# One core's decoder layer: q and k weights read in blocks of 128 input rows that alternate with v, sums of squares by products with ones, and GpSimd in the normalization of x

## The chip, the core and the metric

The kernel runs on one core of a Trainium2 chip as one program. The core has TensorE (PE, matrix products), VectorE (DVE), ScalarE (ACT), GpSimd (POOL) and SyncE (SP), which issues most of the transfers from device memory. Each engine works through its own instructions in program order and waits on semaphores for the others. The metric is the device time of one execution in microseconds (us); the median of several runs counts.

## The reference, cut to what matters

256 tokens of width 1024 go through one layer:

```python
mod = silu(c) @ mod_w + mod_b              # sh1, sc1, g1, sh2, sc2, g2
h   = rmsnorm(x, norm1_g) * (1 + sc1) + sh1
q, k, v, g_dn, r, conv_b, conv_c, conv_h, gate_a, gate_c = split(h @ w_in)
log_a = log_sigmoid(g_dn @ gate_w2 + gate_b) / 16
o = rmsnorm(gla_chunked(q, k, v, log_a)) * silu(r)      # 4 heads, chunks of 64
y = sigmoid(gate_a) * (o @ w_gla_out) + sigmoid(gate_c) * (conv(...) @ w_conv_out)
x = x + g1 * (y @ w_out)
x = x + g2 * hier_moe(rmsnorm(x, norm2_g) * (1 + sc2) + sh2)   # 64 experts
out = rmsnorm(x, final_norm_g)
```

All values are float32. A product of float32 quality is made from three products of split operands: each operand is cut into a high part and a low part, and high x high, high x low and low x high are added.

## The kernel before

**The work list.** The projections are 88 items, each a block of 128 partitions x 1024 float32 (512 KB) of weights. Items 0 to 15 are v, q and k; item 16 on are r, c, h, b, a, g, A, C and O, four blocks each half. For every item ACT casts the block to its high part (`split_h`, L304), DVE subtracts to get the low part (`split_l`, L311), and PE then runs the item's products: 12 of 512 columns for a v block (`mm_v`, L337), 24 of 256 columns for any other (`mm_half`, L328; `mm_blk`, L320). Splits are written five items ahead of the products (LA = 5), and the split buffers hold six items.

**The steps of x.** Eight steps k = 0 to 7, one for each 128 rows of the model width. `h_mod(k)` lets DVE multiply two blocks of mod_w by silu(c) and sum along the row (`mod_blk`, L226); ACT turns the sums into scale and shift, forms h (L256) and casts its high part (L257); DVE forms the low part (`h_lo`, L260). `xnorm(k)` multiplies x by the reciprocal root of its mean square (L245). In `prep(b)` a v item calls `h_mod`, then `split_l` of the item ahead of it, `split_h` of its own, `xnorm` of the next step and `h_lo`. Before, four v items (each with its step) are followed by two q and two k items, and that twice.

**The sums of squares.** DVE squares the first half of x and ACT the second; DVE adds the eight pieces by three additions, PE multiplies by a column of ones, ACT takes the root of the 128x2 result, DVE its reciprocal, and PE spreads it by two transposes.

**Buffers.** Weights come through a ring of 12 blocks: SP issues the next transfer when a block has been used. Accumulators lie in eight PSUM tiles, M0 to M3 and Z0 to Z3. `zt()` hands out the Z tiles in rotation, one for two items; a tile that comes round again can be written only when its last reader has finished. The tile of r's first two items (16 and 17) is read by `r_evac`, which ACT runs in loop 23 (`pre(b + 5)`), and the tile comes round again for item 24.

**The gate and the attention.** From `g_dn` a chain leads to the decays: `gate0`, `gate1` (PE, L380 and L390), absolute value and minimum, exp, ln (ACT), a running sum (DVE, L409), three more exps (`gate5`, `gate8`, ACT, L412, L422, L423). Then come `k_evac`, `q_evac` (DVE) and the attention (`gla_*`). A table of `at`, `first` and `pre` lines says in which loop b each piece is written. MODS spreads the later `mod_blk` calls over loops 19 to 65.

**The rest.** After the items come the router and 16 groups of experts, whose 403 MB of weights are read once.

Of the kernel before, what the change touches and what calls it, by code (L numbers as in the profile page):

```python
# [16 lines left out]
D = 1024  # L17
# [12 lines left out]
WARM = (4, 2)  # L30
XS = 38
# [63 lines left out]
def trunk_kernel(ctx: ExitStack, tc: tile.TileContext, xT: bass.AP, c: bass.AP, modw: bass.AP,  # L95
# [32 lines left out]
    worder = ["v0", "v1", "q", "k", "r0", "r1", "c0", "c1", "h0", "h1", "b0", "b1",  # L128
# [12 lines left out]
    for j in range(len(items) + LA):  # L141
        if j < len(items):
            kind, n, i = items[j]
            if kind[0] == "v":
                o = 2 * (kind == "vB")
# [60 lines left out]
    onesb = sm.tile([128, 128], BF, name="onesb")  # L206
    V.memset(onesb, 1.0)
# [36 lines left out]
    def xnorm(k):  # L244
        V.tensor_mul(xnt[:, k], xres[:, k], rstd1 if k else pr1[:, :TOK])  # L245
# [28 lines left out]
    rc = sm.tile([128, TT], F32, name="rc")  # L274
    S.activation(rc, ps[:, :, 0], AF.Sqrt, bias=epsc, scale=1.0 / D)
# [5 lines left out]
    V.reciprocal(rc, rc)  # L281
    pr1 = mt()
    for tt in range(TT):
        T.transpose(pr1[:, 128 * tt:128 * tt + 128], rc[:, tt:tt + 1].to_broadcast([128, 128]), ident)
    rstd1 = scr2
    S.copy(rstd1, pr1[:, :TOK])
    mod_blk(1, 0)
    xnorm(0)
# [34 lines left out]
    def mm_half(b, kind, i, pb):  # L323
        t = sp(b).rearrange("p s (j k m) -> p s j k m", j=2, k=4)
        for j in range(2):
            for k in range(4):
                for n, (ws, rs) in enumerate(PASSES):
                    T.matmul(pb[i % 2][:, j], t[:, ws, j, k], hl[rs][:, k + 4 * (i // 2)],  # L328
                             start=(kind[1] == "A" and j == 0 and k == 0 and n == 0),
                             stop=(kind[1] == "B" and j == 1 and k == 3 and n == 2), skip_group_check=True)  # L330
# [10 lines left out]
    def prep(b):  # L341

        kind, n, i = items[b]
        k = 4 * (kind == "vB") + i
        if kind[0] == "v":
            h_mod(k)
        if b > 0:
            split_l(b - 1)
        split_h(b)
        if kind[0] == "v":  # L350
            if k < KT - 1:
                xnorm(k + 1)
            h_lo(k)
# [177 lines left out]
    def o_split(h, f):  # L531
        if f is put_h and h == 0:
            L["ohl"] = big.tile([128, 2, KT, TOK], F32R, name="ohl", tag="T10")
        f(L["ohl"], L["o"][:, 2 * h:2 * h + 2], slice(2 * h, 2 * h + 2))


    def conv_tap0(s):
        for k in range(s.start, s.stop):
            S.activation(L["cu"][:, 1, k], L["cu"][:, 0, k], AF.Identity, scale=colt[:, CCW + 16 + k:CCW + 17 + k])

    def conv_taps(s):
        for k in range(s.start, s.stop):
            u, t = L["cu"][:, 0, k], L["cu"][:, 1, k]
# [24 lines left out]
    first(15, gate_abs)
    pre(15, gate_min)
    first(16, gate2)  # L570
    first(17, gate3)
    at(17, gate4)
    at(18, gate6)
    first(19, gate5)
    first(20, gate8)
    at(20, gate7)
    at(20, lambda: k_evac(0))
    at(21, lambda: k_evac(1))
    at(22, lambda: q_evac())
    at(22, gla_setup)  # L580
    at(24, gla_kst)
    at(25, gla_attn)
    first(25, gla_kst2)
    pre(26, gla_attn2, 0)
    pre(26, gla_attn2, 1)
    at(26, gla_state, 0, 1)
    first(27, gla_state2, 0)
    pre(27, gla_state2, 1)
    at(28, gla_state, 2)
    pre(29, gla_state2, 2)  # L590
    at(30, gla_o, 0)
    at(30, gla_o, 1)
    first(31, gla_o2, 0)
    first(31, gla_o2, 1)
    at(31, gla_o, 2)
    at(31, gla_o, 3)
    first(32, gla_o2, 2)
    first(32, gla_o2, 3)
    at(33, gla_ss)
    first(34, gla_ss2)  # L600
    pre(35, gla_ss3)
    at(36, gla_ss4)
# [101 lines left out]
    def evac(b, kind, n, i, ps):  # L704
        if kind[0] in "vqk":
            return
# [11 lines left out]
        elif kind == "c":  # L718
            if q == 0:
                pre(b + 5, conv_setup)  # L720
            pre(b + 5, c_evac, s, ps)
        elif kind == "h":
            V.tensor_mul(L["cu"][:, 0, s], L["cu"][:, 0, s], ps)
# [48 lines left out]
    for b in range(LA, nb):  # L772
        if items[b][0][0] not in "vqk":
            ahead.setdefault(b - (LA if b // 2 <= XS + 2 else LA - 2), []).append(b)
    for b, (kind, n, i) in enumerate(items):
        if i % 2 == 0 and kind[0] not in "vqk":
            ps = (zt(), zt()) if n == "O1" and i == 2 else zt()
        nxts = ahead.get(b, ())
        early = b + LA < nb and items[b + LA][0][0] in "vqk"
# [13 lines left out]
        if kind[0] == "v":  # L793
            mm_v(b, 4 * (kind == "vB") + i, pv)
        elif kind[0] in "qk":
            mm_half(b, kind, i, pq if kind[0] == "q" else pk)
# [375 lines left out]
def layouts(inp):  # L1172
# [21 lines left out]
    win += [w[:, 512 * i:512 * i + 512].reshape(2, 4, 128, 4, 128).transpose(2, 0, 3, 1, 4).reshape(128, 4096)  # L1194
# [37 lines left out]
```

## Time and profile before

| | |
|---|---|
| median of 3 runs (lowest to highest) | 1229.81 us (1229.1 to 1230.33) |
| the profiled execution's own time | 1230.86 us |
| its span, first to last instruction | 1229.0 us |
| busy: PE, DVE, ACT, POOL | 904.5, 379.5, 223.1, 3.9 us |
| moved by DMA | 478.36 MB, 389 GB/s over the span |

Busy time is an average over stages with different limits, so each stage is read by itself. A timeline row gives the start, the busy time of the merged instructions, the engine, the line, the operation, output<-input, the shape and the count; in brackets the idle time ahead of it and what ended it. A busy PE isn't PE at its peak: the rows merge products whose ends are modelled.

### The profile page before, as it was taken

Reading aid. Unit: us, or ns where it says so; the run is one execution under the profiler, and the core shown is the slowest. Engines: PE = TensorE matmul, PEld = TensorE weight load, DVE = VectorE, ACT = ScalarE, POOL = GpSimd, SP = SyncE. Lnnn points to the kernel's source line nnn. Section 1 sums busy time; section 2 is a strip of 40 time slices with the busy share of each in tenths; the row PEclk is TensorE's granted clock in tenths of the full one; section 3 lists DMA queues with packets and bytes.
Section 4 is the critical chain, followed back from the end, with each engine's and each line's share of the span. In section 5 each row is a group of like instructions: output and inputs, shape, how many; then the busy total and the mean of one; then the engine's idle time right before and its main releaser. Section 6 shows DMA issues by size and latency. Waiting matters only on the chain. (4 is left out here: it accounts for less than half of the span.)

```text
span 1229.0 us, 14492 instructions
## 1 busy us (share of the span) xinstructions
PE 904.5 (74%) x6135; PEld 475.6 (39%) x6135; DVE 379.5 (31%) x712; ACT 223.1 (18%) x370; POOL 3.9 (0%) x15
## 2 busy tenths in 40 slices
PE   6999999999788757576666666565756566757665
PEld 3999999998333313121212121221212111412111
DVE  7968799654421202020111111110202001202003
ACT  5674555443211001010101010100000000100002
POOL 0000000000000000000000000000000000000000
PEclk9999999999889888788978788888789887989787
DMA  9978859877999999999999999999999999999996
GB/s 361 406 240 290 269 186 344 342 273 294 401 404 427 428 428 428 428 428 428 427 428 428 428 427 427 428 428 428 427 428 427 429 427 427 426 428 428 427 415 226
DMA packets 56087, 478.36 MB, mean 389 GB/s; under 512 B 5969, under 2 KB 10193, under 8 KB 32338
## 3 DMA queue, kind: packets, MB, share of 16 engines
q1 hardware_dynamic: 54866, 475.56, 94.6%
q10 hardware_dynamic: 1152, 1.83, 0.4%
q8 instruction: 50, 0.82, 0.3%
q14 instruction: 19, 0.16, 0.0%
HBM read 476.31 MB, written 1.05 MB: 388 GB/s over the span
## 5 line engine op out<-in xcount | busy, mean ns | idle before, releaser
L993 PE MATMUL a<-unit,xt 128*32 128x512 f32 x1424 | 208.7, 717 | 103.6 <-DMA unit<-in_ew_dram 102.9
L993 PE MATMUL a<-unit,gt 128*32 128x512 f32 x672 | 112.2, 803 | 68.5 <-DMA unit<-in_ew_dram 65.6
L993 PEld LDWEIGHTS a<-unit,xt 128*32 128x32 f32 x1424 | 43.9, 122 | 253.7 <-DMA unit<-in_ew_dram 135.0
L320 PE MATMUL z<-hhl,sp 128*128 128x256 f32 x1152 | 140.4, 284 | 0.0
L320 PEld LDWEIGHTS z<-hhl,sp 128*128 128x128 f32 x1152 | 138.8, 192 | 1.1 <-issue 0.7
L969 ACT ACTIVATE xt<-m,modc,A 128x128 f32<-128x128 f32 x64 | 25.8, 454 | 534.3 <-PE m L965 534.3
L311 DVE TENSOR_TENSOR sp<-ring,sp 128x1024 fp32r<-128x1024 f32 x88 | 106.7, 1221 | 47.2 <-ACT sp L304 41.7
L993 PE MATMUL a<-ring,xt 128*32 128x512 f32 x624 | 88.7, 694 | 39.9 <-DMA ring<-in_ew_dram 39.8
L304 ACT CAST sp<-ring 128x1024 fp32r<-128x1024 f32 x88 | 90.9, 1047 | 96.2 <-PE z L320 65.2
L1021 DVE TENSOR_TENSOR wk<-wk,m 128x512 f32<-128x512 f32 (+1 forms) x66 | 44.4, 672 | 203.3 <-PE m L1020 203.2
L1011 DVE TENSOR_TENSOR xt<-a,xt 128x1024 f32<-128x1024 f32 (+2 forms) x18 | 19.9, 1106 | 273.5 <-PE a L993 264.3
L993 PEld LDWEIGHTS a<-unit,gt 128*32 128x32 f32 x672 | 22.2, 130 | 144.7 <-DMA unit<-in_ew_dram 91.4
L965 PEld LDWEIGHTS m<-Pm,wk 128*128 128x128 f32 x512 | 60.4, 196 | 21.4 <-issue 21.4
L965 PE MATMUL m<-Pm,wk 128*128 128x128 f32 x512 | 64.0, 284 | 4.7 <-DVE Pm L958 4.4
L1001 DVE TENSOR_TENSOR gt<-gt,a 128x512 f32<-128x512 f32 x16 | 11.0, 688 | 176.4 <-ACT gt L1000 176.4
L1020 PE MATMUL m<-xt,pwt 128*128 128x512 f32 (+1 forms) x132 | 62.8, 618 | 3.3 <-DVE xt L1011 3.3
L993 PE MATMUL a<-ring,gt 128*32 128x512 f32 x288 | 46.3, 774 | 25.2 <-DMA ring<-in_ew_dram 23.6
L226 DVE SCALAR_TENSOR_TENSOR xt<-ring,xt 128x1024 f32<-128x1024 f32 x48 | 58.6, 1221 | 0.6
L993 PEld LDWEIGHTS a<-ring,xt 128*32 128x32 f32 x624 | 18.4, 119 | 100.0 <-DMA ring<-in_ew_dram 58.2
L971 DVE TENSOR_SCALAR xt<-m,A,modc 128x128 f32<-128x128 f32 x64 | 23.3, 406 | 106.2 <-PE m L965 106.2
L1000 ACT ACTIVATE gt<-a 128x512 f32<-128x512 f32 x16 | 9.6, 597 | 229.6 <-PE a L993 229.6
L1020 PEld LDWEIGHTS m<-xt,pwt 128*128 128x128 f32 x132 | 25.1, 203 | 46.7 <-issue 36.7
(245 smaller groups left out, 620.1 us busy)
## 6 DMA issues: line engine op xcount, KB each, us to landing
unit<-in_ew_dram SPq DMA_DIRECT2D x131, 2048.0 KB, 39.1
ring<-in_ew_dram SPq DMA_DIRECT2D x54, 2048.0 KB, 39.1
ring<-in_win_dram SPq DMA_DIRECT2D x88, 512.0 KB, 6.6
ring<-in_modw_dram SPq DMA_DIRECT2D x48, 512.0 KB, 6.2
ring<-in_ew_dram SPq DMA_DIRECT2D x16, 512.0 KB, 7.7
unit<-in_ew_dram SPq DMA_DIRECT2D x4, 1024.0 KB, 34.8
unit<-in_ew_dram SPq DMA_DIRECT2D x4, 512.0 KB, 11.0
xt<-in_xT_dram SPq DMA_DIRECT2D x2, 512.0 KB, 5.0
```

What stands on the lines that cost most here:

```text
L226: V.scalar_tensor_tensor(scr, st.block("m", i, b), 1.0, cB, op0=OP.mult, op1=OP.mult, accum_out=modc[:, 4 * i + b:4 * i + b + 1])
L304: S.copy(sp(b)[:, 0], st.block("w", n, i))
L311: V.tensor_sub(t[:, 1], st.block("w", n, i), t[:, 0].bitcast(F32))
L320: T.matmul(ps, t[:, ws, k], rhs[rs][:, k], start=(clear and k == 0 and n == 0), stop=(k == KT - 1 and n == 2), skip_group_check=True)
L965: T.matmul(ps[:, j], h2[:, tt, f:f + 128], Pm[:, tt], start=(tt == 0), stop=(tt == 1))
L969: S.activation(xg[:, k], ps[:, j], AF.Identity, bias=B2[:, k:k + 1], scale=A2[:, k:k + 1])
L971: V.tensor_scalar(xg[:, k], ps[:, j], A2[:, k:k + 1], B2[:, k:k + 1], op0=OP.mult, op1=OP.add)
L993: T.matmul(ps[32 * j:32 * j + 32, 512 * hh:512 * hh + 512], lhsT[:, 32 * j:32 * j + 32], w[:, j, 512 * hh:512 * hh + 512], start=first, st ...
L1001: V.tensor_mul(gt, gt, ps[:, 512:1024])
L1011: V.tensor_mul(X["y"][:, c0:c1], ps[:, c0:c1], X["g2r"][:, c0:c1])
L1020: T.matmul(ps[:, :w], pwt[:, tt], X["y"][:, s], start=True, stop=True)
L1021: V.tensor_add(acc[:, tt, s], acc[:, tt, s], ps[:, :w])
```

## The change

- The q and k weights are laid out in one block for 128 input rows (as v's are), and the items alternate: v of step 0, qk of step 0, v of step 1, and so on. `mm_qk` multiplies all eight heads of q and k with one row of h. The pieces of the gate and the attention move three loops later (two at `o_norm` and `o_split`), and so do the small loads; `r_evac` and MODS keep their loops.
- The sums of squares come from eight float32 products of 256 columns with a matrix of ones, and root and reciprocal are then taken of 128x256. Three groups of products with ones in bfloat16 (4, 4 and 8 of 512 columns) are put ahead of, between and behind.
- `xnorm(k)` for k > 0 runs on GpSimd, all seven in a row as soon as the reciprocal is there.
- The transfers of c and of x's second half are issued by ACT.
- The convolution's tile `cu` lies in `gb` (T10), and `ohl` in T11. `gate1` skips one Z tile.

```diff
+START = (4, 4, 8)
-    for half, vn in (("A", "v0"), ("B", "v1")):
-        items += [("v" + half, vn, i) for i in range(4)]
-        items += [(n + half, n, i + 2 * (half == "B")) for n in "qk" for i in range(2)]
+    for k in range(KT):
+        items += [("v", f"v{k // 4}", k % 4), ("qk", f"qk{k // 4}", k % 4)]
...
-        nc.sync.dma_start(xres[:, 4 * i:4 * i + 4], xT[:, 4 * i:4 * i + 4])
+        (S if i else nc.sync).dma_start(xres[:, 4 * i:4 * i + 4], xT[:, 4 * i:4 * i + 4])
...
+    def start_warm(n):
+
+        for _ in range(n):
+            T.matmul(cold, onesb, onesb[:, None, :].to_broadcast([128, 4, 128]), start=True, stop=True)
...
     def xnorm(k):
-        V.tensor_mul(xnt[:, k], xres[:, k], rstd1 if k else pr1[:, :TOK])
+        (G if k else V).tensor_mul(xnt[:, k], xres[:, k], rstd1)
...
-    for n in (4, 2, 1):
-        V.tensor_add(xnt[:, 0:n], xnt[:, 0:n], xnt[:, n:2 * n])
-    ps = mt(2, 256)
-    for tt in range(TT):
-        T.matmul(ps[:, tt, 0:1], xnt[:, 0, 128 * tt:128 * tt + 128], onec, start=True, stop=True)
...
+    start_warm(START[1])
+    ps = mt()
+    for k in range(KT):
+        T.matmul(ps[:, :TOK], onesf, xnt[:, k], start=(k == 0), stop=(k == KT - 1))
+    start_warm(START[2])
+    rstd1 = scr2
+    S.activation(rstd1, ps[:, :TOK], AF.Sqrt, bias=epsc, scale=1.0 / D)
...
     mod_blk(0, 0)
...
     mod_blk(1, 0)
-    xnorm(0)
+    V.reciprocal(rstd1, rstd1)
+    for k in range(KT):
+        xnorm(k)
...
+    def mm_qk(b, kk):
+        t = sp(b).rearrange("p s (h m) -> p s h m", h=2 * H)
+        for h in range(2 * H):
+            pb = (pq, pk)[h // H][h % H // 2]
+            for n, (ws, rs) in enumerate(PASSES):
+                T.matmul(pb[:, h % 2], t[:, ws, h], hl[rs][:, kk],
+                         start=(kk == 0 and h % 2 == 0 and n == 0),
+                         stop=(kk == KT - 1 and h % 2 == 1 and n == 2), skip_group_check=True)
...
         split_h(b)
-        if kind[0] == "v":
-            if k < KT - 1:
-                xnorm(k + 1)
-            h_lo(k)
+        if kind == "v":
+            h_lo(b // 2)
...
         L["pg", i] = ps
+        rot["z"] += i
...
-    at(13, gate0)
-    first(14, gate0b)
-    at(14, gate1, 0)
-    at(14, gate1, 1)
+    at(16, gate0)
+    first(17, gate0b)
+    at(17, gate1, 0)
+    at(17, gate1, 1)
...
-    first(20, gate8)
+    first(23, gate8)
```

On DVE the rows of one step k in the middle of items 0 to 15 read so before (sp is a split buffer, t the normalized x or h, hhl the split h):

```order
L226 SCALAR_TENSOR_TENSOR xt,modc<-ring,xt 128x1024 x2
L311 TENSOR_TENSOR sp<-ring,sp 128x1024
L245 TENSOR_TENSOR t_119<-xt,scr_116 128x256
L260 TENSOR_TENSOR hhl<-t_119,hhl 128x256
L226 SCALAR_TENSOR_TENSOR xt,modc<-ring,xt 128x1024 x2
```

And so in the change, where lines are 4 to 8 further down:

```order
L234 SCALAR_TENSOR_TENSOR xt,modc<-ring,xt 128x1024 x2
L315 TENSOR_TENSOR sp<-ring,sp 128x1024
L268 TENSOR_TENSOR hhl<-t_124,hhl 128x256
L315 TENSOR_TENSOR sp<-ring,sp 128x1024
L234 SCALAR_TENSOR_TENSOR xt,modc<-ring,xt 128x1024 x2
```

The first split of a step is now that of the qk block of the step before; the normalization has left the row, and the split of the step's own v block stands ahead of the next step's two mod blocks, not behind them.

On ACT, at the end of the gate's chain, before (the first two rows are `gate5`, the next exps `gate8`; L702 is `r_evac`):

```order
L412 ACT_TABLE_LOAD
L412 ACTIVATE t_158<-t_158 128x1024
L304 CAST sp<-ring 128x1024
L422 ACTIVATE t_158<-t_158 128x1024
L423 ACTIVATE gb<-gb 128x1024
L304 CAST sp<-ring 128x1024 x4
L702 ACT_TABLE_LOAD
L702 ACTIVATE t_158<-z 128x512
```

The same place in the change:

```order
L414 ACT_TABLE_LOAD
L414 ACTIVATE t_180<-t_180 128x1024
L308 CAST sp<-ring 128x1024
L424 ACTIVATE t_180<-t_180 128x1024
L425 ACTIVATE gb<-gb 128x1024
L308 CAST sp<-ring 128x1024
L703 ACT_TABLE_LOAD
L703 ACTIVATE t_180<-z 128x512
```

Four casts, that is three to four items of PE, stood between `gate8` and `r_evac`; now one does.

On PE from `gate1` (L390) to the attention's first transposes (L440), before; L328 is an item of q or k, L320 of r and what follows, 24 products each:

```order
L390 MATMUL z<-e_71 128x256 x4
L328 MATMUL m<-hhl,sp 128x256 x48
L320 MATMUL z<-hhl,sp 128x256 x192
L440 MATMUL m<-ident,gb 128x128 x8
L320 MATMUL z<-hhl,sp 128x256 x24
```

And in the change from the last qk item on, with `gate0` as L381, `gate1` as L391 and the transposes as L442:

```order
L332 MATMUL m<-hhl,sp 128x256 x24
L381 MATMUL z<-t_124,e_71 32x256 x8
L324 MATMUL z<-hhl,sp 128x256 x24
L391 MATMUL z<-e_71 128x256 x4
L324 MATMUL z<-hhl,sp 128x256 x240
L442 MATMUL m<-ident,gb 128x128 x8
```

Ten items stood between `gate1` and the end of item 23; now seven do (17 to 23). The transposes stood ahead of item 24; now they stand three items later.

## Rows read from the trace of the kernel before

**Rows 1.** Stretches: length, busy us of PE, PEld, DVE, ACT, POOL, PEclk, DMA share, GB/s

```profile
160.00:180.00 20.00, 20.00 (x169) 20.00 (x169) 18.68 (x29) 10.24 (x13) 0.00 (x0) 1.00 0.61 192
340.00:700.00 360.00, 248.70 (x1578) 79.00 (x1576) 55.00 (x124) 21.39 (x47) 0.00 (x0) 0.84 1.00 426
```

**Rows 2.** Timeline of PE, 0 to 110 us

```profile
2.44 3.75 PE L264 MATMUL m<-e,onesf 1*128 1x512 f32 x4 [2.44 <-DMA e<-in_c_dram]
...
16.05 2.07 PE L337 MATMUL z<-sp,hhl 128*128 128x512 f32 x4 [2.99 <-ACT sp L304]
...
32.31 11.68 PE L328 MATMUL m<-hhl,sp 128*128 128x256 f32 x96
43.82 11.07 PE L337 MATMUL z<-sp,hhl 128*128 128x512 f32 x48
...
57.69 1.07 PE L380 MATMUL z<-t,e 128*32 128x256 f32 x16
...
61.66 1.89 PE L390 MATMUL z<-e 128*128 128x256 f32 x8
63.20 6.10 PE L328 MATMUL m<-hhl,sp 128*128 128x256 f32 x48
69.14 23.20 PE L320 MATMUL z<-hhl,sp 128*128 128x256 f32 x192
92.18 1.04 PE L440 MATMUL m<-ident,gb 128*128 128x128 f32 x8
```

**Rows 3.** Timeline of all engines, 0 to 45 us: the start

```profile
7.17 1.06 ACT L267 ACTIVATE t<-xt 128x1024 f32<-128x1024 f32 x1 [0.35 <-DMA xt<-in_xT_dram]
...
13.09 0.37 ACT L286 COPY scr<-m 128x256 f32<-128x256 f32 x1 [1.05 <-PE m L284]
...
13.49 0.42 DVE L245 TENSOR_TENSOR t<-xt,m 128x256 f32<-128x256 f32 x1
...
14.95 1.04 ACT L304 CAST sp<-ring 128x1024 fp32r<-128x1024 f32 x1
```

**Rows 4.** The same timeline: one step of items 0 to 3

```profile
19.69 1.22 DVE L226 SCALAR_TENSOR_TENSOR xt<-ring,xt 128x1024 f32<-128x1024 f32 x1
...
22.10 1.22 DVE L311 TENSOR_TENSOR sp<-ring,sp 128x1024 fp32r<-128x1024 f32 x1
...
23.49 1.04 ACT L304 CAST sp<-ring 128x1024 fp32r<-128x1024 f32 x1
23.62 0.43 DVE L260 TENSOR_TENSOR hhl<-t,hhl 128x256 fp32r<-128x256 f32 x1
23.96 1.22 DVE L226 SCALAR_TENSOR_TENSOR xt<-ring,xt 128x1024 f32<-128x1024 f32 x1
```

**Rows 5.** Lines L508 and L433: ns least/median/most, first and last start

```profile
L508 DVE RECIPROCAL scr<-scr x1: 1745/1745/1745, 140.3 to 140.3; 128x256 f32<-128x256 f32 x1
...
L433 POOL MEMSET gc<- x1: 958/958/958, 80.6 to 80.6; 128x1024 f32 x1
```

**Rows 6.** Timeline of ACT, 56 to 93 us

```profile
80.44 1.28 ACT L412 ACT_TABLE_LOAD   x1 [3.91 <-DVE t L409]
...
84.59 1.04 ACT L423 ACTIVATE gb<-gb 128x1024 f32<-128x1024 f32 x1
...
90.49 1.28 ACT L702 ACT_TABLE_LOAD   x1
91.79 0.60 ACT L702 ACTIVATE t<-z 128x512 f32<-128x512 f32 x1
```

**Rows 7.** Stretches around the router, columns as in group 1

```profile
324.00:326.00 2.00, 0.94 (x12) 0.04 (x4) 1.79 (x9) 0.57 (x2) 0.00 (x0) 1.00 0.97 401
326.00:328.00 2.00, 0.00 (x0) 0.00 (x0) 1.79 (x16) 0.00 (x0) 0.00 (x0) 0.95 0.96 410
336.00:338.00 2.00, 2.00 (x13) 0.34 (x6) 0.00 (x0) 0.00 (x0) 0.00 (x0) 0.50 1.09 467
338.00:340.00 2.00, 2.00 (x19) 2.00 (x20) 0.04 (x1) 0.81 (x2) 0.00 (x0) 0.99 0.93 397
```

More of the change, by code (lines that the diff above doesn't have):

```diff
@@ L125, in fl @@
         return t.rearrange("p a b -> p (a b)")
-    worder = ["v0", "v1", "q", "k", "r0", "r1", "c0", "c1", "h0", "h1", "b0", "b1",
+    worder = ["v0", "v1", "qk0", "qk1", "r0", "r1", "c0", "c1", "h0", "h1", "b0", "b1",
               "a0", "a1", "g0", "g1", "A0", "A1", "C0", "C1", "O0", "O1"]
@@ L143, in trunk_kernel @@
             kind, n, i = items[j]
-            if kind[0] == "v":
-                o = 2 * (kind == "vB")
+            if kind == "v":
+                o = 2 * int(n[1:])
                 blocks += [(("m", o, i), modw[o, :, 1024 * i:1024 * i + 1024]),
@@ L193, in trunk_kernel @@
     G.iota(jp, pattern=[[1, 128]], base=0, channel_multiplier=-1)
+    onesb = sm.tile([128, 128], BF, name="onesb")
+    V.memset(onesb, 1.0)
     onesf = sm.tile([128, 128], F32, name="onesf")
     V.memset(onesf, 1.0)
+    cold = zt(512)
+    def start_warm(n):
+        for _ in range(n):
+            T.matmul(cold, onesb, onesb[:, None, :].to_broadcast([128, 4, 128]), start=True, stop=True)
+    start_warm(START[0])
     epsc = sm.tile([128, 1], F32, name="epsc")
@@ L205, in trunk_kernel @@
     V.tensor_scalar(tri, jp, 0.0, None, op0=OP.is_gt)
-    onesb = sm.tile([128, 128], BF, name="onesb")
-    V.memset(onesb, 1.0)
     io = sm.tile([128, 128], F32, name="io")
@@ L280, in trunk_kernel @@
     mod_blk(0, 0)
[L281 to L286, printed above, removed]
     mod_blk(1, 0)
-    xnorm(0)
+    V.reciprocal(rstd1, rstd1)
+    for k in range(KT):
+        xnorm(k)
     spt = [big.tile([128, 2, 2, 1024], F32R, name="sp", tag=t) for t in SPLIT]
@@ L321, in mm_blk @@
                          stop=(k == KT - 1 and n == 2), skip_group_check=True)
[L323 to L330, printed above, removed]
+    def mm_qk(b, kk):
[6 more added lines that the diff above has]
+                         stop=(kk == KT - 1 and h % 2 == 1 and n == 2), skip_group_check=True)
     def mm_v(b, kk, pv):
@@ L343, in prep @@
         kind, n, i = items[b]
-        k = 4 * (kind == "vB") + i
-        if kind[0] == "v":
-            h_mod(k)
+        if kind == "v":
+            h_mod(b // 2)
         if b > 0:
@@ L349, in prep @@
         split_h(b)
-        if kind[0] == "v":
-            if k < KT - 1:
-                xnorm(k + 1)
-            h_lo(k)
+        if kind == "v":
+            h_lo(b // 2)
     def small_loads():
@@ L532, in o_split @@
         if f is put_h and h == 0:
-            L["ohl"] = big.tile([128, 2, KT, TOK], F32R, name="ohl", tag="T10")
+            L["ohl"] = big.tile([128, 2, KT, TOK], F32R, name="ohl", tag="T11")
         f(L["ohl"], L["o"][:, 2 * h:2 * h + 2], slice(2 * h, 2 * h + 2))
@@ L538, in conv_tap0 @@
         for k in range(s.start, s.stop):
-            S.activation(L["cu"][:, 1, k], L["cu"][:, 0, k], AF.Identity, scale=colt[:, CCW + 16 + k:CCW + 17 + k])
+            S.activation(cu1[:, k], cu0[:, k], AF.Identity, scale=colt[:, CCW + 16 + k:CCW + 17 + k])
     def conv_taps(s):
         for k in range(s.start, s.stop):
-            u, t = L["cu"][:, 0, k], L["cu"][:, 1, k]
+            u, t = cu0[:, k], cu1[:, k]
             for j in (1, 0):
@@ L559, in pre @@
         todo.setdefault((i, "pre"), []).append((f, a))
-    at(1, small_loads)
-    at(12, late_loads)
-    first(12, lambda: v_evac())
-    at(13, gate0)
-    first(14, gate0b)
-    at(14, gate1, 0)
-    at(14, gate1, 1)
[L568 to L574, printed above, removed]
-    first(20, gate8)
[L576 to L602, printed above, removed]
+    at(8, small_loads)
+    at(14, late_loads)
+    first(15, lambda: v_evac())
+    at(16, gate0)
+    first(17, gate0b)
+    at(17, gate1, 0)
+    at(17, gate1, 1)
+    first(18, gate_abs)
+    pre(18, gate_min)
+    first(19, gate2)
+    first(20, gate3)
+    at(20, gate4)
+    at(21, gate6)
+    first(22, gate5)
+    first(23, gate8)
+    at(23, gate7)
+    at(23, lambda: k_evac(0))
+    at(24, lambda: k_evac(1))
+    at(25, lambda: q_evac())
+    at(25, gla_setup)
+    at(27, gla_kst)
+    at(28, gla_attn)
+    first(28, gla_kst2)
+    pre(29, gla_attn2, 0)
+    pre(29, gla_attn2, 1)
+    at(29, gla_state, 0, 1)
+    first(30, gla_state2, 0)
+    pre(30, gla_state2, 1)
+    at(31, gla_state, 2)
+    pre(32, gla_state2, 2)
+    at(33, gla_o, 0)
+    at(33, gla_o, 1)
+    first(34, gla_o2, 0)
+    first(34, gla_o2, 1)
+    at(34, gla_o, 2)
+    at(34, gla_o, 3)
+    first(35, gla_o2, 2)
+    first(35, gla_o2, 3)
+    at(36, gla_ss)
+    first(37, gla_ss2)
+    pre(38, gla_ss3)
+    at(39, gla_ss4)
     for h in range(H):
-        at(38 + 2 * h, o_norm, h)
-        at(40 + 2 * h, o_split, h, put_h)
-        at(41 + 2 * h, o_split, h, put_l)
+        at(40 + 2 * h, o_norm, h)
+        at(42 + 2 * h, o_split, h, put_h)
+        at(43 + 2 * h, o_split, h, put_l)
     for b, ms in mod_at.items():
@@ L663, in trunk_kernel @@
     ps = None
-    def conv_setup():
-        L["cu"] = big.tile([128, 2, KT, TOK], F32, name="cu", tag="T11")
+    cu1, cu0 = (gb[:, 2 * i:2 * i + 2].rearrange("p a h t -> p (a h) t") for i in range(2))
     def c_evac(s, ps):
-        S.copy(L["cu"][:, 0, s], ps)
+        S.copy(cu0[:, s], ps)
     def q_evac():
@@ L682, in b_evac @@
             L["chl"] = big.tile([128, 2, KT, TOK], F32R, name="chl", tag="T9")
-        x = L["cu"][:, 1, 2 * q:2 * q + 2]
+        x = cu1[:, 2 * q:2 * q + 2]
         V.tensor_mul(x, x, ps)
@@ L687, in b_high @@
         s = slice(2 * q, 2 * q + 2)
-        put_h(L["chl"], L["cu"][:, 1, s], s)
+        put_h(L["chl"], cu1[:, s], s)
     def b_low(q):
         s = slice(2 * q, 2 * q + 2)
-        put_l(L["chl"], L["cu"][:, 1, s], s)
+        put_l(L["chl"], cu1[:, s], s)
         if q == 3:
-            st.free("T11")
+            st.free("T10")
     def v_evac():
@@ L704, in evac @@
     def evac(b, kind, n, i, ps):
-        if kind[0] in "vqk":
+        if kind in ("v", "qk"):
             return
@@ L718, in evac @@
         elif kind == "c":
[L719 to L720 removed]
             pre(b + 5, c_evac, s, ps)
         elif kind == "h":
[L723 removed]
+            V.tensor_mul(cu0[:, s], cu0[:, s], ps)
             at(b + 1, conv_tap0, s)
@@ L736, in evac @@
             if q == 3:
-                st.free("T10")
+                st.free("T11")
         elif kind == "C":
@@ L772, in trunk_kernel @@
     for b in range(LA, nb):
-        if items[b][0][0] not in "vqk":
+        if items[b][0] not in ("v", "qk"):
             ahead.setdefault(b - (LA if b // 2 <= XS + 2 else LA - 2), []).append(b)
     for b, (kind, n, i) in enumerate(items):
-        if i % 2 == 0 and kind[0] not in "vqk":
+        if i % 2 == 0 and kind not in ("v", "qk"):
             ps = (zt(), zt()) if n == "O1" and i == 2 else zt()
         nxts = ahead.get(b, ())
-        early = b + LA < nb and items[b + LA][0][0] in "vqk"
+        early = b + LA < nb and items[b + LA][0] in ("v", "qk")
         run((b, "first"))
@@ L783, in trunk_kernel @@
         for nxt in nxts:
-            if items[nxt - 1][0] == "kB":
+            if items[nxt - 1][0] == "qk":
                 split_l(nxt - 1)
@@ L792, in trunk_kernel @@
         run(b)
[L793 to L796, printed above, removed]
+        if kind == "v":
+            mm_v(b, b // 2, pv)
+        elif kind == "qk":
+            mm_qk(b, b // 2)
         else:
@@ L1193, in layouts @@
            for i in range(2)]
-    win += [w[:, 512 * i:512 * i + 512].reshape(2, 4, 128, 4, 128).transpose(2, 0, 3, 1, 4).reshape(128, 4096)
+    win += [w[512 * i:512 * i + 512, 0:1024].reshape(4, 128, D).transpose(1, 0, 2).reshape(128, 4096)
             for i in range(2)]
```

4 lines of the change are left out of this document (1 added, 3 removed).

## The prediction

> **What bounds the kernel now.** I read the stretches first. From about 340 us on the transfers run at 426 GB/s with a DMA share of 1.00, while PE is busy for 249 of 360 us; before that, as in 160 to 180 us, PE is busy for the whole stretch and DMA for 61% [rows 1]. So the projections are bound by PE and the experts by their transfers, and these wait for ring blocks and tiles that the projections free. Whatever moves the end of the projections moves the long transfer stretch by as much. The question is only when PE gets through its list.
>
> The timeline of PE answers it for the kernel before. PE starts item 0 at 16.05 us, ends item 15 at 69.14, with `gate0` (57.69) and `gate1` (61.66) inside, and ends item 23 at 92.18 [rows 2]. A v item takes 12 x 11.07 / 48 = 2.77 us, an item of 24 products of 256 columns 24 x 23.20 / 192 = 2.90 [rows 2]. Sixteen items would take 8 x (2.77 + 2.90) = 45.4; with the 1.07 of `gate0` and the 1.54 from 61.66 to 63.20 of `gate1` 48.0. PE took 53.1 from 16.05 to 69.14, so its early stalls and slow products hold 5.1 us. That is what alternating can win at most, if PE starts no earlier.
>
> **The start.** I call X0 the moment at which `xnorm(0)` starts: 13.49 before. From there to the end of the first cast is 2.50 (14.95 + 1.04) [rows 3], and that path stays. In the change PE first runs four products with ones (about 1.9, by the four at 16.05 in 2.07), so the products of c end near 6.8 instead of 6.19 [rows 2]. The second silu and ACT's square (1.06, ended at 8.23 before [rows 3]) follow. Four more products with ones and the eight of the sums come next. `gate1` took 1.89 for four float32 products of 256 columns [rows 2], so eight take 3.8 and the four with ones 0.9: they end near 11.3. The root of 128x256 on ACT goes by the copy of that shape, 0.37 [rows 3]. The reciprocal of 128x256 takes 1.75 [rows 5]; it was 128x2 before. X0 is 11.3 + 0.4 + 1.7 = 13.4, no gain. The bounds: 11.9 if PE catches up with ACT's square, 18.3 if all of it runs at half the clock. I take a value near the lower one, since PE works almost without a pause from 1.2 us on. What the three additions and two transposes cost is given back by the reciprocal.
>
> **The pace of the steps.** In the step before, the first mod block starts at 19.69, the first split at 22.10 (two mod blocks, 2.41), ACT's cast of the v block at 23.49, `h_lo` at 23.62 [rows 4]. Put the change's order on these: the cast of v ends 4.84 after the step's start; DVE, which has done `h_lo` by 4.36, waits for it and splits v from 4.88. The split takes 1.14 to the next start (1.22 less some 0.08 of overlap, as `h_lo`'s 0.43 gives 0.34 to the next start [rows 4]). The next step starts after 6.02. PE needs 2.77 + 2.90 = 5.67, so DVE and ACT's chain set the pace, not PE. The normalization that leaves DVE wins nothing here: `h_lo` waits for ACT's cast of h, and 0.42 of DVE lay under that wait.
>
> The first mod block of step 1 starts at X0 + 2.50 + 0.04 + 1.14 = X0 + 3.68. Step 7 starts six paces later, at X0 + 39.8. Behind it come the split of step 6's qk block (ends 2.41 + 1.22 = 3.63 later), 22 of its 24 products (2.66), item 14 (2.77) and item 15 (2.90): item 15 ends at X0 + 51.8 = 65.2. A low clock at the first items is hidden, since PE is ahead of DVE's pace by 0.35 a step.
>
> **Seven items instead of ten.** `gate0` (1.07) and item 16 (2.90) end at 69.2. Then `gate1` (1.54) and items 17 to 23 (7 x 2.90): PE could start item 24 at 91.0, where it stood at 92.18 before. The front is worth 1.1 us.
>
> But item 24 writes the Z tile that item 16 filled, and `r_evac` must have read it. Before, ACT finished `gate8` at 84.59 + 1.04 = 85.63, 23.97 after `gate1` began at 61.66; the chain waited only at its start for PE and once for DVE's running sum (3.91) [rows 2, 6]. Four casts later `r_evac` ran from 90.49 to 92.39; the attention's transposes filled PE from 92.18 on, so the wait was covered [rows 2, 6]. In the change the chain starts with `gate1` at 69.2 and takes the same 23.97, since the same operations in the same order depend on the same offsets of PE's items. One cast (1.04 [rows 4]), the table load (1.28) and the silu (0.60) follow: 69.2 + 26.9 = 96.1. PE reaches item 24 at 91.0 and finds nothing else to do: 5.1 us of idle time. The cover, three items and the transposes, is gone. Queued behind on ACT are the casts of items 29 and 30, which PE doesn't need yet.
>
> **What follows the idle time.** [...] I charge 4 us of work at half the clock, 2.0 lost; the bounds are 0 and 5.1, half of the low stretch from 327.8 to 338, and since part of that stretch was idle I stay below the middle. Further on, two mod blocks (2.41 [rows 4]) now stand on DVE ahead of the attention's masked copy, for which PE waits; bounds 0 and 2.4, I take 0.5, since most of an item of PE covers them.
>
> **GpSimd.** No row has a product on GpSimd. Its largest memset, four times as wide, took 0.96 [rows 5]. A fourth of it, 0.24, and all of it are the bounds for one of the seven; a product reads two operands and writes one, so I take 0.7. Their results are needed a step apart and are in time either way. If they don't disturb DVE, the price is 0; if each holds DVE up for its length at the upper bound, 6.7. Three of the seven fall into DVE's waits before step 1, and of the other four I charge half: 1.4.
>
> The seven operations lie where DVE sets the pace, so a hold-up would be paid in full. [...]
>
> The moved transfers of c and x cost ACT two more issues, before its first work. `cu` and `ohl` trade tiles, and both are freed at the same items as before; I cost that at nothing, because the same number of tiles is freed in the same order.
>
> **The sum.** -1.1 (front) + 5.1 (item 24) + 2.0 (clock) + 0.5 (attention) + 1.4 (GpSimd) = +7.9. Against the profiled execution's own 1230.86 that is 1238.8; that execution is 1.05 above the median of the runs shown, so I predict 1229.81 + 7.9 = 1237.7.
>
> **The rivals.**
> - *The chain is in time.* If `r_evac` ends within 21.8 of `gate1`'s start instead of 26.9, item 24 doesn't wait and the clock stays. This takes away 7.1: 1230.6, not slower; with X0 at its lower bound 1229.1, and from there on each further part that costs less than charged (GpSimd 1.4, attention 0.5) carries it below 1227.3, to faster. For it: the margin before can't be read closely, since the transposes hid it. Against it: three table loads and the scan are in the chain whatever PE does. Chance 0.25, of which 0.13 end faster by over 0.2% and 0.11 within it.
> - *The wait without the clock.* PE idles 5.1 but keeps its clock: 1235.7. The clock at the router fell after a shorter pause, which speaks against it. Chance 0.15.
> - *GpSimd holds DVE up in full.* Each of the seven products takes DVE's turn for its 0.7 us, 4.9 in all, or up to 6.7: 1241.2 to 1243. Against it: DVE waits for ACT twice in a step. [...] Chance 0.15.
> - *PE sets the pace of the steps.* If DVE's step is 5.67 or less, item 15 ends up to 2.1 earlier: 1235.6, or 1234.2 if GpSimd's price is hidden too. Chance 0.10. The change would then win what alternating is able to win, and lose it at item 24.
>
> The forecast itself keeps 0.35; its own range, with the bounds of X0, the clock and GpSimd, is 1234 to 1241.
>
> **How the numbers follow.** Fast and slow cases lie on one side except for the chain in time, so the range reaches down into it: 1228.5 to 1242 leaves out about 0.13 below and 0.06 above. A difference of 0.2% (2.5 us) is about what a measurement of this kernel can tell from none. Faster: 0.13. Within 0.2%: 0.12, almost all from the chain in time. Slower: 0.75.
>
> **What the profile of the changed kernel would show.** X0 near 13.4 and the reciprocal at 1.7; steps that start 6.0 apart; item 15's end near 65 to 66.5; PE idle for some 5 us ahead of item 24 with ACT's `r_evac` as the releaser, ACT having gone from `gate8` through one cast to the table load; a granted clock of 0.50 after it; the experts' transfers at 426 GB/s, as long as before and some 8 later. The prediction is wrong if there is no idle time between items 16 and 40, if X0 lies beyond 15, or if the transfers start later without PE being later.

## The result

The changed kernel takes 1237.91 us (median of 4; 1237.8 to 1240.42) against 1229.45 (median of 4), 8.5 us more; the ratio is 1.0072, 95% interval 1.006 to 1.0084. The profiled execution took 1237.93, its span is 1236.1. The forecast was 1237.7. The main wait and its mechanism were right, one term had the wrong sign, and that the figure fits so well is chance, as the parts show.

The two stretches of [rows 1], after the change (columns as there):

```profile
160.00:180.00 20.00, 20.00 (x163) 19.79 (x162) 18.23 (x28) 9.22 (x13) 0.00 (x0) 1.00 0.51 154
340.00:700.00 360.00, 247.12 (x1592) 81.26 (x1596) 57.86 (x137) 23.70 (x52) 0.00 (x0) 0.86 1.01 428
```

The limits are the same: PE in the projections, transfers in the experts. PE's timeline, with the rows that answer to [rows 2]:

```profile
8.39 4.75 PE L280 MATMUL m<-t,onesf 128*128 128x256 f32 x16
...
18.09 5.49 PE L341 MATMUL z<-sp,hhl 128*128 128x512 f32 x12 [3.23 <-ACT sp L308]
...
68.78 1.07 PE L381 MATMUL z<-t,e 128*32 128x256 f32 x16
...
72.75 1.89 PE L391 MATMUL z<-e 128*128 128x256 f32 x8
74.29 20.50 PE L324 MATMUL z<-hhl,sp 128*128 128x256 f32 x168
99.53 10.33 PE L324 MATMUL z<-hhl,sp 128*128 128x256 f32 x72 [4.75 <-ACT t L703]
109.70 1.03 PE L442 MATMUL m<-ident,gb 128*128 128x128 f32 x8
...
118.19 2.74 PE L467 MATMUL m<-t,gc 64*128 64x256 f32 x16
```

Item 15 ends at 68.78, items 16 to 23 and the gate's products end at 94.8, and there PE stops: item 24 waits 4.75 us for `r_evac` (L703). ACT's timeline shows why it is late (compare [rows 6]):

```profile
91.44 1.28 ACT L414 ACT_TABLE_LOAD   x1 [3.85 <-DVE t L411]
...
95.60 1.04 ACT L425 ACTIVATE gb<-gb 128x1024 f32<-128x1024 f32 x1
96.54 1.03 ACT L308 CAST sp<-ring 128x1024 fp32r<-128x1024 f32 x1
97.59 1.28 ACT L703 ACT_TABLE_LOAD   x1
98.88 0.60 ACT L703 ACTIVATE t<-z 128x512 f32<-128x512 f32 x1
```

One cast stands between `gate8` and the table load, and `r_evac` ends at 99.48, 26.7 after `gate1` began at 72.75. At the end of the pause the granted clock falls from 1.00 to 0.50 (column PEclk) and comes back:

```profile
98.00:100.00 2.00, 0.47 (x2) 0.47 (x3) 2.00 (x4) 1.99 (x3) 0.00 (x0) 0.85 0.48 166
100.00:102.00 2.00, 2.00 (x11) 2.00 (x11) 1.67 (x3) 0.41 (x1) 0.00 (x0) 0.50 0.74 238
102.00:104.00 2.00, 2.00 (x16) 2.00 (x15) 2.00 (x4) 0.00 (x0) 0.00 (x0) 0.79 0.62 162
104.00:106.00 2.00, 2.00 (x19) 2.00 (x19) 0.91 (x3) 1.54 (x2) 0.00 (x0) 1.00 0.67 199
```

The 72 products from 99.53 to 109.70 took 10.2; at a PEclk of 1.00 three items take 8.7 (2.90 each [rows 2]). So 1.5 are lost.

The start on PE, DVE and GpSimd; the last row has the lengths of GpSimd's seven products (ns least/median/most):

```profile
6.71 1.89 PE L203 MATMUL z<-onesb 128*128 128x512 bf16 x4
...
12.97 1.89 PE L203 MATMUL z<-onesb 128*128 128x512 bf16 x8
...
13.68 1.75 DVE L290 RECIPROCAL scr<-scr 128x256 f32<-128x256 f32 x1 [0.50 <-ACT scr L283]
15.54 0.42 DVE L253 TENSOR_TENSOR t<-xt,scr 128x256 f32<-128x256 f32 x1
15.68 9.24 POOL L253 TENSOR_TENSOR t<-xt,scr 128x256 f32<-128x256 f32 x7 [11.71 <-DVE scr L290]
...
19.22 1.75 DVE L234 SCALAR_TENSOR_TENSOR xt<-ring,xt 128x1024 f32<-128x1024 f32 x1
...
22.57 1.74 DVE L315 TENSOR_TENSOR sp<-ring,sp 128x1024 fp32r<-128x1024 f32 x1
23.20 1.72 POOL L253 TENSOR_TENSOR t<-xt,scr 128x256 f32<-128x256 f32 x1
24.24 0.96 DVE L268 TENSOR_TENSOR hhl<-t,hhl 128x256 fp32r<-128x256 f32 x1
...
26.26 1.21 DVE L234 SCALAR_TENSOR_TENSOR xt<-ring,xt 128x1024 f32<-128x1024 f32 x1
...
L253 POOL TENSOR_TENSOR t<-xt,scr x7: 716/1710/1789, 15.7 to 23.2; 128x256 f32<-128x256 f32 x7
```

X0 is 15.54, not 13.4. The first step lasts 26.26 - 19.22 = 7.04, the later ones 6.08.

Against the kernel before, PE has done item 23 2.6 later (94.78 for 92.18), waits 4.75, loses 1.5 to the clock and 0.7 at L467 (2.74 for 2.00): 9.6. The first expert product comes at 320.38 for 310.76. In the kernel before:

```profile
100.68 2.00 PE L465 MATMUL m<-t,gc 64*128 64x256 f32 x16
...
310.76 1.92 PE L993 MATMUL a<-unit,xt 128*32 128x512 f32 x16 [0.55 <-ACT xt L969]
```

and in the changed one:

```profile
320.38 1.92 PE L992 MATMUL a<-unit,xt 128*32 128x512 f32 x16 [0.55 <-ACT xt L968]
```

Yet the span is only 7.1 longer. Two questions were left: are these waits what the change costs, and where do 2.5 come back?

### The profile page after: what moved, and what is told of

It is laid out like the page before. It is cut to its first block, busy times and chain, and to the rows that moved or that the text cites. A ratio compares the mean times of both kernels' runs of the same rounds, so it can differ in the third digit from the quotient of the medians.

```text
span 1236.1 us, 14548 instructions
## 1 busy us (share of the span) xinstructions
PE 910.8 (74%) x6161; PEld 481.8 (39%) x6161; DVE 379.6 (31%) x702; ACT 222.7 (18%) x369; POOL 13.2 (1%) x22
## 5 line engine op out<-in xcount | busy, mean ns | idle before, releaser
L992 PE MATMUL a<-unit,gt 128*32 128x512 f32 x672 | 108.1, 777 | 64.4 <-DMA unit<-in_ew_dram 59.3
```

The costliest lines, as they stand in the source:

```text
L992: T.matmul(ps[32 * j:32 * j + 32, 512 * hh:512 * hh + 512], lhsT[:, 32 * j:32 * j + 32], w[:, j, 512 * hh:512 * hh + 512], start=first, st ...
```

## The experiments

Each is told by its ratio to the kernel before, run beside it on the same chip. "Router" is the start of the first expert product in the trace, "rest" what lies from there to the end of the span.

| | ratio, interval | router | rest |
|---|---|---|---|
| before | 1 | 310.76 | 918.2 |
| changed | 1.0072, 1.006 to 1.0084 | 320.38 | 915.7 |
| E1 | 1.0078, 1.0065 to 1.0092 | 318.06 | 917.5 |
| E2 | 1.0092, 1.0079 to 1.0106 | 319.52 | 917.5 |
| E3 | 1.0077, 1.0063 to 1.0091 | 319.92 | 916.2 |
| E4 | 1.0004, 0.9995 to 1.0014 | 310.77 | 917.7 |
| E5 | 1.0086, 1.0072 to 1.0099 | 321.16 | 917.4 |
| E6 | 1.0084, 1.0071 to 1.0098 | 319.35 | 917.5 |
| E7 | 1.0053, 1.004 to 1.0067 | 317.17 | 917.9 |
| E8 | 1.004, 1.0026 to 1.0054 | 315.23 | 917.0 |
| E9 | 1.0031, 1.002 to 1.0042 | 314.21 | 915.7 |
| E10 | 0.9985, 0.9977 to 0.9994 | 308.77 | 917.6 |
| E11 | 1.0094, 1.0079 to 1.0109 | 320.34 | 915.7 |

**E1, r copied out of its tiles.**

```diff
+    def r_copy(q, ps):
+        V.tensor_copy(L["sr"][:, 2 * q:2 * q + 2], ps)
...
         if kind == "r":
+            if q < 2:
+                at(21, r_copy, q, ps)
+                ps = L["sr"][:, 2 * q:2 * q + 2]
             pre(b + 5, r_evac, q, ps)
```

> Start from the changed kernel (1237.9). DVE copies r's first two pairs out of their Z tiles at loop 21, and silu then runs in place from SBUF, so item 24 no longer waits for ACT's chain. If the wait (4.75) and the low clock behind it (1.5) are what the change loses there: 1237.9 - 6.2 = 1231.7, the 72 products behind the transposes' place at full clock. Rival, the wait only moves (to item 26, to the transposes or to the masked copy): 1236 to 1238, with an idle time of PE of 3 us or more between 94 and 125. Rival, the clock falls for another reason than the idle time: 1233.2, with 0.50 still there near 100.

The wait at item 24 and the low clock there are gone (PEclk is 1.00 from 90 to 130), the router comes 2.3 earlier, and no time is won that could be measured; 1231.7 was forecast. PE's timeline shows two new waits:

```profile
106.39 1.09 PE L442 MATMUL m<-ident,gb 128*128 128x128 f32 x8 [3.06 <-DVE gb L673]
...
116.63 1.99 PE L467 MATMUL m<-t,gc 64*128 64x256 f32 x14 [1.00 <-DVE gc L459]
```

L673 is `q_evac`. Why do the transposes of k wait for q? `mt()` hands out M0 to M3 in rotation. Before, it had been called four times when the transposes came (twice for c, for the sums, for the spread reciprocal), and they took M0 and M1, k's accumulators. The new sums of squares call it three times: the transposes get M3, q's, which DVE reads last. The rival, that the wait moves, holds.

**E2, normalization on DVE.**

```diff
-        (G if k else V).tensor_mul(xnt[:, k], xres[:, k], rstd1)
+        V.tensor_mul(xnt[:, k], xres[:, k], rstd1)
...
         if kind == "v":
+            if b // 2 < KT - 1:
+                xnorm(b // 2 + 1)
             h_lo(b // 2)
```

> Start from the changed kernel (1237.9). All eight normalizations on DVE, each placed ahead of the low part of h as before the change; GpSimd does nothing in the steps. If GpSimd's price is the longer first step (7.04 against 6.08): 1236.9, X0 unchanged near 15.5, all steps 6.1. Rival, DVE sets the pace with every operation that it has: seven times 0.42 are added and the 1.0 comes off, 1239.9, steps of 6.5. Rival, GpSimd costs nothing in the end since PE is behind: 1237.9.

Every step takes 6.02 and item 15 ends at 67.35, 1.43 earlier. Of these, 1.0 is the first step (7.04 before the edit), in which GpSimd worked beside DVE. Another 0.3 are the five steps that follow (6.08 before the edit, with GpSimd done at 24.9), and 0.1 is X0, 15.42, which precedes GpSimd's first product. So GpSimd's own price is 1.0 rather than 1.4, and seven products of 0.42 on DVE cost nothing. Item 24 waits 4.8 all the same, the 72 products behind it take 10.7 instead of 10.2 at their low clock, and at the router 0.9 is left; in the time nothing shows, where 1236.9 was forecast.

**E3, the start as before** (SP issues c and x, sums by additions, a column of ones and transposes, START at zero).

> Start from the changed kernel (1237.9). The start as before: SP issues c and both halves of x, the sums of squares by three additions, a column of ones and two transposes, no products with ones ahead. If the new start is what makes X0 late: X0 near 13.5 and 2.1 less, 1235.8. Rival, the steps are bound behind X0 by something else (blocks of the ring, PE at a low clock at its first items): X0 earlier but item 15 ends where it did, 1237.9.

X0 is 14.12 (13.5 was forecast; the second half of x landed later than in [rows 3], and ACT's square ended at 8.86). Item 15 ends 1.06 earlier (67.72), the 72 products at item 24 take 10.8 instead of 10.2, and 0.5 is left at the router. The time is the same, where 1235.8 was forecast. With E2 and E7 the start's worth can be read without GpSimd: E7's item 15 ends at 65.19, E2's at 67.35, 2.2 apart, and so are their X0, 13.25 and 15.42.

**E4, the kernel before with the ring begun at another block.**

```diff
-        st.bfree(i)
+        st.bfree((i + 1) % NB)
```

> The kernel before (1229.5) with one edit: the twelve ring blocks are first filled from block 1 on, not from block 0, which gives the experts' units the order over tiles and ring that they have in the changed kernel. If that order is where the change gets back some 2.5 us of the 9.6 by which it is late at the router: 1227.0 to 1227.7, without the dip of the transfers at 352 to 356. Rival, the changed kernel gets it back by being late (transfers closer behind what frees their tiles): 1229.5.

SP then issues the experts' transfers in the changed kernel's order of tiles and ring. Nothing changes: my theory of the regained 2.5 falls.

**E5, the changed kernel again.**

> The changed kernel unaltered, on the chip of the next three. 1.0072 times the kernel before, first expert product at 320.4, item 24 waits 4.7. In the changed kernel's first trace PE went from the first expert product to the act of group 0 in 35.4 us; the kernel before took 37.4, and the three variants of the first call 37.3 to 37.5, with the clock at 0.50 near 351 where the changed kernel had 1.00. If those 2.0 belong to that one execution, it is 37.4 here; if they belong to the program, 35.4 again.

The same 4.75 at item 24, but the 72 products behind it take 11.5 here, not 10.2, and the router comes 0.8 later than in the first trace, though X0 (15.05) is earlier. From the router to the act of group 0 (PE's transposes for it, L1003 in the changed kernel) this trace takes 37.5, where the first took 35.4, and so it gives nothing back; its span is 1238.6. The column "rest" has two heaps: 915.7 in three traces (the changed kernel, E9, E11), which take 35.4 to that act, and 917.0 to 918.2 in the others, which take 37.3 to 37.5. E3, with 916.2, takes 37.4 too and gains further on, at a place not traced. The clock tells the heaps apart. The changed kernel's first trace around the act of group 0:

```profile
350.00:352.00 2.00, 0.43 (x3) 0.14 (x1) 1.76 (x6) 0.08 (x1) 0.00 (x0) 1.00 1.01 426
352.00:354.00 2.00, 1.88 (x17) 0.56 (x17) 0.06 (x1) 0.37 (x1) 0.00 (x0) 1.00 0.98 418
354.00:356.00 2.00, 0.56 (x6) 0.26 (x3) 0.69 (x1) 0.60 (x1) 0.00 (x0) 1.00 1.00 426
```

and E1's:

```profile
350.00:352.00 2.00, 1.81 (x10) 0.51 (x13) 0.29 (x1) 0.37 (x1) 0.00 (x0) 0.69 1.04 442
352.00:354.00 2.00, 2.00 (x12) 0.22 (x4) 0.00 (x0) 0.00 (x0) 0.00 (x0) 0.50 0.94 401
354.00:356.00 2.00, 0.58 (x8) 0.42 (x4) 0.69 (x1) 0.60 (x1) 0.00 (x0) 0.96 0.97 410
```

PE's products there are short and broken by waits, and ahead of the act the granted clock falls a second time behind the router in some traces (0.50 in 352 to 354 in E1) and not in others (1.00 there in the changed kernel's first trace); by the two heaps that moves the end by some 2. The same program shows both (the changed kernel and E5), so it belongs to the single execution and not to the change.

**E6, the copies and one M tile skipped** (E1, and `rot["m"] += 1` behind the sums).

> Start from the changed kernel. The copies of r's first two pairs as in the run before, and one M tile skipped after the sums, so that the attention's transposes take the tiles of k's accumulators again, as they did before the change, and not one of q's, which DVE reads 7 us later. If the wait of 3.1 at the transposes came from the shifted rotation: no idle time of PE between items 16 and 30, the first expert product at 313.3 (320.4 less 4.75, 1.5 and 0.8), and a time 4 to 6 below the changed kernel's. Rival, the transposes wait for k's own products instead, which DVE ends near 102.9: 1 us gained at most against the run with the copies alone (first expert product at 318.1).

The transposes start at 103.05 without a wait, 6.65 earlier than in the changed kernel, and then PE waits for the masked copy:

```profile
111.54 0.70 PE L468 MATMUL m<-t,gc 64*128 64x256 f32 x2
116.47 3.43 PE L468 MATMUL m<-t,gc 64*128 64x256 f32 x14 [4.24 <-DVE gc L460]
```

DVE between `q_evac` (ends at 106.2) and the copy, the first mod block and the last rows:

```profile
107.22 1.22 DVE L234 SCALAR_TENSOR_TENSOR xt<-ring,xt 128x1024 f32<-128x1024 f32 x1
...
114.55 1.23 DVE L234 SCALAR_TENSOR_TENSOR xt<-ring,xt 128x1024 f32<-128x1024 f32 x1
115.70 0.08 DVE L234 DVE_READ_ACCUMULATOR xt<-ring,xt 128x1 f32 x1
115.70 1.32 DVE L460 COPY_PREDICATED gc<-cmask,m 128x512 f32<-128x512 int32 x2
```

Five mod blocks and three splits lie there. The attention went three loops later, the mod blocks stayed, and so they are now ahead of it. The clock falls behind this wait too (0.50 in 116 to 118). The rotation was the cause at the transposes, as stated, but the forecast (no idle time, the router at 313.3) failed: the wait moved to a third place.

**E7, what is left is the alternation** (the start of E3, DVE of E2, the copies of E1).

> Start from the changed kernel: the start as before, normalization on DVE, and the copies of r (the M rotation is then that of before by itself). What stays of the change is the alternation. By the sum of the parts: first expert product at 313.3 less 0.9 (GpSimd) less 1.1 (start) = 311.3, 0.5 later than before; the time within 1.5 us of the kernel before. Rival, alternating itself is worth the 5.1 of early stalls: 307 and 4 us faster. Rival, some part hides another: 313 or later, 2 us slower or more.

PE reaches the transposes at 99.68; less the three items that now stand ahead of them (8.7) that is 91.0, 1.2 earlier than in [rows 2]. Then it waits 4.3 for the masked copy. So the rival holds that one part hides another: the router comes at 317.17, where 311.3 was forecast.

**E8, E7 with the cast of v first.**

```diff
         if kind == "v":
+            split_h(b)
             h_mod(b // 2)
         if b > 0:
             split_l(b - 1)
-        split_h(b)
+        if kind != "v":
+            split_h(b)
```

> The run before this one with one more edit: in a step ACT casts the v block ahead of its work on h, not behind it, so that DVE's split of v needs no wait. If the pace of 6.08 is DVE and ACT's chain: steps of 5.7, set by PE, item 15 2.3 us earlier, the first expert product near 309, and about 1.5 to 2.5 below the run without the edit. Rival, PE or the ring's transfers set the pace: steps of 6.0 and no gain.

One step's end on DVE in E7 (low part of h, split of v, the next mod block):

```profile
26.89 0.43 DVE L268 TENSOR_TENSOR hhl<-t,hhl 128x256 fp32r<-128x256 f32 x1
27.84 1.23 DVE L321 TENSOR_TENSOR sp<-ring,sp 128x1024 fp32r<-128x1024 f32 x1 [0.52 <-ACT sp L314]
28.98 1.22 DVE L234 SCALAR_TENSOR_TENSOR xt<-ring,xt 128x1024 f32<-128x1024 f32 x1
```

and in E8:

```profile
26.83 0.43 DVE L268 TENSOR_TENSOR hhl<-t,hhl 128x256 fp32r<-128x256 f32 x1
27.17 1.22 DVE L321 TENSOR_TENSOR sp<-ring,sp 128x1024 fp32r<-128x1024 f32 x1
28.31 1.22 DVE L234 SCALAR_TENSOR_TENSOR xt<-ring,xt 128x1024 f32<-128x1024 f32 x1
```

The wait of 0.52 is gone, DVE needs 5.42 a step, PE goes through items 1 to 15 without a pause, and item 15 ends 1.75 earlier (63.44). That DVE and ACT's chain set the pace is shown. The router, forecast near 309, comes only at 315.23, since PE still waits 4.3 for the masked copy.

**E9, the three waits together** (E6, and the first seventeen of MODS raised by 3).

> Start from the changed kernel: the copies of r, the skipped M tile, and the first seventeen of the mod blocks three loops later, as the attention's pieces are. If the masked copy that PE waited 4.2 for in the run without the third edit was late because of the mod blocks ahead of it on DVE: no idle time of PE between items 16 and 40, the clock at 1.00 there, first expert product at 313 (319.4 less 4.2 and some 2.2 of low clock), and the time 5 to 7 below the changed kernel's, some 1.003 times the kernel before. Rival, the wait moves once more (to the decays' sums or the attention's output): 316 to 319.

```profile
74.67 29.14 PE L325 MATMUL z<-hhl,sp 128*128 128x256 f32 x240
103.66 1.04 PE L443 MATMUL m<-ident,gb 128*128 128x128 f32 x8
...
112.15 2.00 PE L468 MATMUL m<-t,gc 64*128 64x256 f32 x16
```

Between items 16 and 40 PE pauses once more, for 0.4 at the spreading of the attention's root (E11 shows that the moved mod blocks bring this wait), and the clock stays at 1.00 over the places above. The router is 6.2 earlier than in the changed kernel and the ratio 1.0031, 5 to 7 us better than the changed kernel's 1.0072 and 1.0086. The new start and the moved normalization are still in it.

**E10, E8 with the mod blocks moved.**

> The run with the cast of v first, and the mod blocks three loops later. By the parts: first expert product at 315.2 less 4.3 and some 2.2 = 308.7, 2 earlier than before the change; 0.997 to 0.999 times the kernel before. Rival, the transfers can't follow: the wait goes, but the end stays at 1.004.

The router comes 2.0 earlier than in the kernel before, as forecast from the parts, and the kernel is 0.15% faster. The cast's place isn't part of the change; E8 gained 1.9 by it at the router (317.17 to 315.23). By this sum, which no run tried, the alternation with the waits removed and the old start and normalization would bring the first expert product at 310.7, where the kernel before has 310.76. Its transfers from 340 to 700 us run as in [rows 1]:

```profile
340.00:700.00 360.00, 253.50 (x1569) 79.75 (x1570) 55.45 (x124) 20.55 (x45) 0.00 (x0) 0.83 1.00 426
```

**E11, the changed kernel with the mod blocks moved alone.**

> The changed kernel with the mod blocks three loops later and nothing else. The wait of 4.7 at item 24 stays and covers the rest; only the 0.7 at the masked copy goes: first expert product at 319.6 to 320.4, 1.006 to 1.009 times the kernel before. Rival, the mod blocks also hold up the gate's chain (the running sum and the split ahead of it): the wait at item 24 is shorter by 1 us or more, and the time with it.

L467 no longer waits (118.27 to 120.2) and PE is 0.7 ahead behind it; item 24 still waits 4.75. The 0.7 doesn't reach the router. All but 0.1 of it is lost at the spreading of the attention's root, for which the changed kernel doesn't wait:

```profile
161.84 1.97 PE L517 MATMUL m<-scr,P 128*128 128x256 f32 x8 [0.39 <-DVE scr L510]
```

The moved mod blocks now lie on DVE ahead of the root's reciprocal (L510).

## Why the prediction came out right

- **Item 24's wait** was forecast at 5.1 and is 4.75; the chain from `gate1` takes 26.7 (forecast 26.9). The chain moves along with PE, so the wait hardly depends on the front: E2, with PE 1.4 earlier there, waits 4.81. The rival of a chain in time is out.
- **The clock behind it**: 2.0 forecast, my estimate from the low stretch at the router, 327.8 to 338 by the means of [rows 7]; 1.5 measured in this trace; with the same wait 2.0 in E2, 2.1 in E3 and 2.8 in E5.
- **The front** was the term that failed: -1.1 forecast, +2.6 measured (+2.1 in E5). Of the 3.7 between, GpSimd had a term of its own, and X0 is 2.1: 15.54 for 13.4. The prediction named X0 beyond 15 as a sign of being wrong, and for this part it was. The step that failed is the claim that the reciprocal gives back what the additions and transposes cost. In it, the products with ones and the sums (0.9 and 3.8) were taken at the pace of [rows 2], 0.23 to 0.24 a product, and they began at about half of it, 0.43 apart up to 10.5. E7 shows the term at its intended size: without the new start and GpSimd the front wins 1.2.
- **Why X0 was late.** The four products with ones at 6.71 take as long, 1.89, as the eight of the same shape at 12.97. Up to 10.5 products with ones and sums alike begin 0.43 apart, from 10.8 on 0.22. PEclk reads 1.00 in this stretch, but the trace has no clock entry before 10.66, where its first, at 1.00, begins. Behind item 24, where PEclk is 0.50, the pace is about half too: products begin 0.21 apart there and 0.12 apart at 1.00. How long the slow stretch lasts differs between traces with this start: the sums begin at 8.42 in E1, 8.40 in E2 and 8.39 here and take 4.12, 4.62 and 4.75, and item 0 starts at 17.49, 17.98 and 18.09. The sums end at 13.14 where 11.3 was forecast, of which 0.2 is a slip (6.8 + 0.9 + 3.8 is 11.5). ACT's square, which the second half of the sums needs, ended at 9.85, 1.6 later than in [rows 3], but it held nothing up: the first product that reads it begins at 11.25.
- **The pace** was forecast at 6.02 and is 6.08; E8 shows that DVE and ACT set it.
- **GpSimd**: 1.4 forecast, 1.0 measured, since E2's 1.43 holds 0.4 that isn't GpSimd's work. The shortest of its products, in a pause of DVE, took 0.72, as assumed; the median is 1.71, more than the upper bound of 0.96, and a mod block took 1.63 to 1.75 for 1.22. The four later products end 0.6 after the end of a DVE operation, and the DVE operation after that ends as if it had begun, at its undisturbed length, 0.13 to 0.15 before the product's end. The last product ends at 24.92, the split before it at 24.31, and `h_lo` at 25.20, which is 0.43 after 24.77. By these ends the two took turns, and the waits stand inside the longer rows. Each turn cost DVE 0.4 to 0.5, 2.0 in all, and half of it fell into DVE's own waits for ACT. The full hold-up of 4.9 didn't come, since the first three of the seven fell mostly into DVE's pauses and the others cost less than their 0.72.
- **The attention**: 0.5 forecast, 0.7 measured, but the bound (0 to 2.4, two mod blocks) was wrong. Behind item 24's wait a second (3.1) and a third (4.2 and a low clock) stood hidden; I counted the mod blocks next to the copy and not the five since `q_evac`, and I didn't follow the M rotation.
- **The end**: the router is 9.6 later, not 7.9, and a shift of the router was to move the end by as much. The span moved by 7.1 since that execution lost less to the clock at group 0; E5 moved by 9.6. So the fit of the figure is luck. Front and GpSimd together came 2.3 later than their two terms, wait and clock were 0.8 shorter, the attention 0.2 longer; 1.7 were missing, and that execution gave 2.5 back. With the router's 9.6 on the median before, 1229.45, the time would be 1239.

So slower was right, and item 24's wait is the largest part of it, as forecast. That the wait is what separates the kernels holds only with the two behind it: taken away alone it wins nothing that can be measured (E1), all three win 5 to 7 us (E9). What E9 leaves, 3.5 at the router, holds the new start and the moved normalization; no run takes away these two and all three waits without moving the cast as well.

## What to carry to other kernels

When pieces are moved by some loops, move with them everything that shares their engine or their buffers' rotation: a schedule table left in place and one allocation less each made a wait nearly as long as the one in view. A wait in the profile may cover others of its size; ask what comes next when it is taken away, and count all of an engine's queue back to the last point where it was in time. Before moving work to an idle engine, look whether the busy one waits there anyway: here DVE had the room.

## What the runs showed of the hardware that was not expected

- In the changed kernel GpSimd's product of 128x256 float32 took 0.72 us in a pause of DVE and 1.71 to 1.79 beside mod blocks, a split and `h_lo` on DVE, which took 0.4 to 0.5 longer than undisturbed (1.63 to 1.75 for 1.22, 1.74 for 1.22, 0.96 for 0.43). By the ends of the rows the two took turns; the profile has this as longer rows and not as idle time.
- At the start of the changed kernel PE's products came at half their later pace (0.43 apart up to 10.5 us, 0.22 from 10.8 on), while PEclk reads 1.00: the trace has no clock entry before 10.66. The pace of equal products tells what the column doesn't.
- In the eight traces in which PE paused 4.2 to 4.8 us for item 24 or for the masked copy, PEclk fell from 1.00 to 0.50 within the pause or at its end. It stayed low for 3.4 us in the changed kernel, E6 and E11, and for 6.8 in E2, E3, E5, E7 and E8; behind item 24's wait that cost 1.5 to 2.8. After the router, where PE works in short pieces, it fell at different places in each execution (in the changed kernel PEclk is below 1.00 in 338 to 346, in E5 in 340 to 348 and again in 354 to 358), which moves the end by some 2 us: differences below that can't be read from single traces here.
